# A decoder layer on one Trainium2 core: the second gate/up pair's a12 b21 right behind the first pair's

## The chip, the cores and the metric

The kernel runs on one core of one Trainium2 chip. The metric is the time of one execution in microseconds on the device, the median of several runs. TensorE (PE in the profile) multiplies; VectorE (DVE), ScalarE (ACT) and GpSimd (POOL) work element by element; SyncE (SP) and POOL issue the transfers. Every engine takes its instructions in the order in which they stand in its queue, and waits on semaphores for what others make.

## What is computed

One decoder layer over 512 tokens and 16 meta tokens, of width 2048: an input projection, stick-breaking attention beside a gated short convolution, an output projection with a residual, and then the part that matters here, a SwiGLU feed-forward of width 5632:

```python
        h = h + o @ w_out[l]

        n2 = _rmsnorm(h, g_ffn[l])
        h = h + (jax.nn.silu(n2 @ w_gate[l]) * (n2 @ w_up[l])) @ w_down[l]
```

All of it is float32. TensorE works on fp32r, so each operand is split into hi (a rounded copy) and lo (what is left), and a product is made of three matmuls: hi·hi, hi·lo and lo·hi.

## The kernel before

**Stages.** Input projection and attention, the convolution, the output projection (mostly `wide_product`, lines 709 to 718), then 44 gate/up pairs, then the down projection.

**Seven products for a pair.** A pair `i` is one tile of 128 columns of w_gate and the same of w_up. With the contraction and the 512 tokens cut in two halves each, it is a 2×2 block product, made of seven block products (`block_product`, line 720) instead of eight. In this text product s takes the activations `acts[s]`, named f0 to f6 in the program, and a weight made of the pair's four quads b11, b12, b21, b22 of 128×1024:

| product | weight | accumulates in |
|---|---|---|
| 0 | b11 | x |
| 1 | t1 = b11 + b12 | z |
| 2 | t2 = t1 + b22 | x |
| 3 | b22 | z |
| 4 | t3 = b12 + b22 | x |
| 5 | b21 (the a12 b21) | y |
| 6 | t2 + b21 | x |

Each is 24 matmuls of 256 columns: for each of eight k, hi with the activation's hi (line 736), hi with its lo (737), lo with its hi (738). x, y and z are PSUM banks, two of each. ACT copies banks between products into `sides` (lines 761 to 765), and DVE forms the results (767, 771, 774).

**The weights' way.** SP loads a quad into its place in `sw_in` (line 613). Of six places of 128×1024 four hold quads, the last two the sums: place 4 has t1/t2 and place 5 t3 in even pairs, the other way round in odd ones. DVE adds (648, and in place 682 and 655). For the split of a weight ACT casts hi (641), and DVE subtracts lo (642), into one of three slots of `sw_split`. A split is therefore issued two products ahead, and its cast waits until the product three before is done. The next pair's quad is loaded as soon as the old one is used up; b12, for instance, behind t3.

**Pair 0** takes its products in the order 5, 0, 1, 2, 3, 4, 6 (`FIRST_ORDER`, line 659), since f5 is complete before the others: the last tile of the output projection is that part of the residual stream which f0 to f4 still need. For that tile DVE makes the residual (832 to 835), ACT the source (836), and DVE and ACT the blocks f0, f1, f2 and the last k of f3 and f4. f3, f4 and f6 come back from DRAM by POOL's loads (880), which may start only when the last product of the output projection is done.

**The scale r_h.** h is not normalised before the products. `h_scale` (line 908) makes the factor r_h of each token from the sum of squares acc_h: ACT and POOL split acc_h into work_r (187, 188), two matmuls ss_h sum over the partitions (500, 501), DVE reads them (502), ACT makes Ln and Exp (194, 195) and POOL four operations (196 to 199), which write r_h over acc_h. It is called inside pair 0, ahead of product 4, under high priority. `gate` then multiplies u and g with r_h on DVE (937, 939) and applies Silu on ACT (940, for which ACT loads a table).

**What sets the order.** The program is written in one order; a scheduler moves instructions within an engine's queue by priority and by its own estimate of when their operands are there. `tc.high_priority` lifts the splits and additions. `tc.keep_in_program_order` and `tc.issue_after` hold an instruction to its place.

## Time and profile before

| | |
|---|---|
| median of 3 runs | 2064.36 us (2063.72 to 2064.47) |
| the profiled execution | 2063.57 us, its span 2061.8 us |
| output projection ends, gate/up begins | 792.8 us |
| stretch 792.80 to 800.00: PE, DVE busy | 5.72 and 6.93 of 7.20 us |
| stretch 800.00 to 816.00: PE, DVE busy | 13.36 and 15.53 of 16.00 us |
| stretch 850.00 to 900.00: PE, DVE busy | 50.00 and 46.53 of 50.00 us |

The stretches are read from the view by windows: the first two are those in which TensorE has gaps, the last is a piece of the gate/up products in their steady course. A row of the timeline is start, duration, engine, line, operation, output and input; in brackets stand the idle time ahead of it and what released it.

### The profile page before, as it was taken

The numbers are of one execution on the slowest core, as the hardware profiler recorded it, in microseconds if no ns is written. First come the engines' busy times: TensorE is split into PE (matmuls) and PEld (weight loads), VectorE is DVE, ScalarE is ACT, GpSimd is POOL, SyncE is SP. The second block draws the span as 40 slices with busy tenths as digits, with TensorE's granted clock in tenths as the row PEclk, the third lists the DMA queues.
The fourth block names the chain that finished last, engine by engine and source line by source line (L and its number), as shares of the span: only waits on it lengthen the run. The fifth ranks groups of instructions, "written<-read, shape, count | busy, mean of one in ns | idle before, by whom it ended". The sixth has DMA issues, their size and how long they took to land.

```text
span 2061.8 us, 39364 instructions
## 1 busy us (share of the span) xinstructions
PE 2048.5 (99%) x16086; PEld 1975.5 (96%) x16086; DVE 1629.3 (79%) x2133; ACT 1016.9 (49%) x1522; POOL 368.6 (18%) x499
## 2 busy tenths in 40 slices
PE   9999999999999999999999999999999999999999
PEld 8899999999998888999999999999999999999999
DVE  7877767533336669999898898898888988888888
ACT  7666566322224344555555555555555544444443
POOL 0111111010104544111111011011011243121111
PEclk9999999999999999999999999999999999999999
DMA  5122222222235667546555555465465899798864
GB/s 198 63 82 73 82 72 83 82 93 92 94 104 176 181 187 240 158 135 194 164 145 172 155 163 165 146 180 153 149 175 160 258 332 348 192 296 211 218 149 94
DMA packets 144117, 330.41 MB, mean 160 GB/s; under 512 B 12400, under 2 KB 62064, under 8 KB 143936
## 3 DMA queue, kind: packets, MB, share of 16 engines
q1 hardware_dynamic: 67456, 212.50, 32.2%
q0 software_dynamic: 76480, 115.40, 21.9%
q8 instruction: 126, 2.06, 0.4%
q14 instruction: 55, 0.45, 0.1%
HBM read 260.74 MB, written 67.11 MB: 159 GB/s over the span
## 4 chain that ended last, share of the span: by engine, by line
PE 96%; DVE 2%; DMA 1%; ACT 1%; issue 0%; SPq 0%; POOL 0%; DVEq 0%; ACTq 0%; POOLq 0%
PE x L738 11%; PE x L736 11%; PE x L737 11%; PE z L736 6%; PE z L737 6%; PE z L738 6%; PE y L736 3%; PE y L738 3%; PE y L737 3%; PE po L716 3%; PE po L717 3%; PE po L715 3%; PE pv L173 2%; PE pu L177 1%; PE pc L173 1%; PE pu L173 1%
## 5 line engine op out<-in xcount | busy, mean ns | idle before, releaser
L641 ACT CAST sw_split<-sw_in 128x1024 fp32r<-128x1024 f32 (+1 forms) x534 | 526.6, 988 | 553.0 <-PE z L737 167.0
L642 DVE TENSOR_TENSOR sw_split<-sw_in,sw_split 128x1024 fp32r<-128x1024 f32 (+1 forms) x534 | 615.1, 1152 | 96.7 <-ACT sw_split L641 93.7
L738 PE MATMUL x<-f,sw_split 128*128 128x256 f32 x1408 | 387.8, 275 | 1.7 <-DVE sw_split L642 1.7
L737 PE MATMUL x<-f,sw_split 128*128 128x256 f32 x1408 | 387.7, 275 | 1.3 <-DVE f L188 1.3
L736 PE MATMUL x<-f,sw_split 128*128 128x256 f32 x1408 | 387.7, 275 | 0.2 <-ACT f L187 0.2
L738 PEld LDWEIGHTS x<-f,sw_split 128*128 128x128 f32 x1408 | 264.4, 188 | 1.9 <-DVE sw_split L642 1.9
L737 PEld LDWEIGHTS x<-f,sw_split 128*128 128x128 f32 x1408 | 264.4, 188 | 1.5 <-DVE f L188 1.5
L736 PEld LDWEIGHTS x<-f,sw_split 128*128 128x128 f32 x1408 | 264.4, 188 | 0.5 <-ACT f L187 0.4
L142 DVE TENSOR_TENSOR wlo<-raw,whi 128x512 fp32r<-128x512 f32 (+1 forms) x198 | 139.8, 710 | 124.9 <-ACT whi L141 124.0
L928 POOL DMA_DIRECT2D fd<-s x147 | 103.7, 922 | 690.0 <-DVE s L188 673.5
L141 ACT CAST whi<-raw 128x512 fp32r<-128x512 f32 (+1 forms) x198 | 121.1, 614 | 180.4 <-PE pu L175 64.5
L736 PE MATMUL z<-f,sw_split 128*128 128x256 f32 x704 | 194.0, 276 | 0.6 <-ACT sides L763 0.6
L738 PE MATMUL z<-f,sw_split 128*128 128x256 f32 x704 | 193.9, 275 | 0.0
L737 PE MATMUL z<-f,sw_split 128*128 128x256 f32 x704 | 193.9, 275 | 0.0
L648 DVE TENSOR_TENSOR sw_in<-sw_in 128x1024 f32<-128x1024 f32 (+1 forms) x144 | 166.1, 1153 | 5.4 <-DMA sw_in<-w_down 1.1
L738 PE MATMUL x<-ring,sw_split 128*128 128x256 f32 x608 | 167.5, 276 | 0.5 <-DVE sw_split L642 0.5
L737 PE MATMUL x<-ring,sw_split 128*128 128x256 f32 x608 | 167.4, 275 | 0.0
L736 PE MATMUL x<-ring,sw_split 128*128 128x256 f32 x608 | 167.4, 275 | 0.0
L736 PEld LDWEIGHTS z<-f,sw_split 128*128 128x128 f32 x704 | 132.2, 188 | 0.8 <-ACT sides L763 0.8
L738 PEld LDWEIGHTS z<-f,sw_split 128*128 128x128 f32 x704 | 132.2, 188 | 0.0
L737 PEld LDWEIGHTS z<-f,sw_split 128*128 128x128 f32 x704 | 132.2, 188 | 0.0
L738 PEld LDWEIGHTS x<-ring,sw_split 128*128 128x128 f32 x608 | 114.2, 188 | 0.7 <-DVE sw_split L642 0.7
(345 smaller groups left out, 5256.2 us busy)
## 6 DMA issues: line engine op xcount, KB each, us to landing
sw_in<-w_gu SPq DMA_DIRECT2D x176, 512.0 KB, 3.9
raw<-w_in SPq DMA_DIRECT2D x92, 512.0 KB, 3.3
fd<-s POOLq DMA_DIRECT2D x147, 256.0 KB, 5.4
sw_in<-w_down SPq DMA_DIRECT2D x96, 384.0 KB, 4.1
ring<-fd POOLq DMA_DIRECT2D x42, 768.0 KB, 17.4
sw_in<-w_out SPq DMA_DIRECT2D x30, 512.0 KB, 3.7
out_T<-d POOLq DMA_DIRECT2D x54, 256.0 KB, 4.7
sw_in<-w_down SPq DMA_DIRECT2D x16, 512.0 KB, 7.7
```

The costliest lines, as they stand in the source:

```text
L141: sc.copy(hi[:, :c], raw)
L142: ve.tensor_tensor(lo[:, :c], raw, hi[:, :c].bitcast(F32), ALU.subtract)
L173: pe.matmul(ps, wh, ah[:, a:b], start=k == 0, stop=False)
L641: sc.copy(hi, src)
L642: ve.tensor_tensor(lo, src, hi.bitcast(F32), ALU.subtract)
L648: ve.tensor_tensor(sums[name], a, b, ALU.add)
L715: pe.matmul(ps, hi[:, kk], ah, start=k == 0, stop=False)
L716: pe.matmul(ps, hi[:, kk], al, start=False, stop=False)
L736: pe.matmul(p, hi[:, kk], act[:, 0, k], start=start and j == k == 0, stop=False, skip_group_check=skip)
L737: pe.matmul(p, hi[:, kk], act[:, 1, k], start=False, stop=False, skip_group_check=skip)
L738: pe.matmul(p, lo[:, kk], act[:, 0, k], start=False, stop=k == n - 1, skip_group_check=skip)
L928: gp.dma_start(fd[c][s][:, :, k], t[:, :, i])
```

## The change

Pair 1's product 5 is made right behind pair 0's product 5, both into their own bank y. Its weight b21 is loaded for that a first time, into place 5 of `sw_in`, which is free until t3 of pair 0; the load stands behind the first four loads of the output projection's weights in the text. b21 of pair 1 is loaded again into its own place, for the addition ahead of product 6. The order of splits is a list, `order_w`: (0,5), (1,5), and then all others pair by pair without product 5 of the first two pairs. For pairs 0 and 1 the addition of b21 moves to product 6.

Two orders of issue are set beside it: t3 of pair 1 is kept in program order, and `h_scale` is issued behind the last load of f6.

```diff
     def add_quads(i, name, a, b):
         n = pairs[i][0]
         sums[name] = w_place(sw_in, n, (4 if n == 8 else 6) + ((name == "t3") ^ i % 2))
-        ve.tensor_tensor(sums[name], a, b, ALU.add)
+        return ve.tensor_tensor(sums[name], a, b, ALU.add)
 
     def add_t3(i, b):
-        add_quads(i, "t3", b["12"], b["22"])
+        t3 = add_quads(i, "t3", b["12"], b["22"])
+        if i == 1:
+            tc.keep_in_program_order(t3)
         load_next(i, "12")
...
-    FIRST_ORDER = (5, 0, 1, 2, 3, 4, 6)
+    EARLY = 2
+    order_w = [(i, 5) for i in range(EARLY)] + [
+        (i, s) for i in range(len(pairs)) for s in range(7) if i >= EARLY or s != 5
+    ]
+
+    def load_early():
+        quads["early"] = w_place(sw_in, 8, 5)
+        nc.sync.dma_start(quads["early"], pairs[1][1][2])
...
-        i, s = divmod(len(split_w) - WIDE, 7)
-        if i == len(pairs):
+        if len(split_w) - WIDE == len(order_w):
             return
+        i, s = order_w[len(split_w) - WIDE]
         n = pairs[i][0]
-        if i == 0:
-            s = FIRST_ORDER[s]
...
             elif s == 5:
-                split_quad(b["21"], n)
-                if i:
+                split_quad(quads["early"] if i == 1 else b["21"], n)
+                if i >= EARLY:
                     add_last(i, b)
             else:
-                if not i:
+                if i < EARLY:
                     add_last(i, b)
...
-        y, z, x = bank("y"), bank("z"), bank("x")
+        y, z, x = early.pop(i, None) or bank("y"), bank("z"), bank("x")
         p1, p5, u2 = side("p1"), side("p5"), side("u2")
         if not i:
             block_product(y, acts[5], True)
+            early[1] = bank("y", 1)
+            block_product(early[1], acts[5], True)
         block_product(x, acts[0], True)
...
-        if i:
+        if i >= EARLY:
             block_product(y, acts[5], True)
         ve.tensor_tensor(c1[:, 0], y, p1, ALU.add)
...
     for _ in range(4):
         load_wide()
+    load_early()
...
-                    gp.dma_start(acts[s][:, part, :n], fx[s][:, part, :n], max_dma_last_dim=4096)
+                    last_f = gp.dma_start(acts[s][:, part, :n], fx[s][:, part, :n], max_dma_last_dim=4096)
...
-        with tc.high_priority(1 << 20):
+        with tc.high_priority(1 << 20), tc.issue_after(last_f.ins):
             token_scale(acc_h, acc_h, D, "h", (w[:, 0], w[:, 1], a[:, 0], a[:, 1], b), gp)
```

What this does to the order of instructions is shown at three places. In names, sw_in and sw_split are the weights before and after the split, a number behind x, z, g or u is the pair, and lines of the changed program are 9 to 15 higher.

ScalarE, from the last cast of f3 and f4 to the copy of product 2, before:

```order
L187 CAST f34_8170<-src7_8118 128x256 x2
L641 CAST sw_split_6910<-sw_in_6909 128x1024
L761 COPY sides_8161<-x0_8227 128x256
L641 CAST sw_split_6910<-sw_in_6909 128x1024
L763 COPY sides_8161<-z0_8226 128x256
L187 CAST work_r_8368<-acc_h_6907 128x512
L641 CAST sw_split_6910<-sw_in_6909 128x1024
L765 COPY sides_8161<-x0_8227 128x256
```

And now:

```order
L187 CAST f34_8169<-src7_8117 128x256 x2
L641 CAST sw_split_6910<-sw_in_6909 128x1024
L187 CAST work_r_8396<-acc_h_6907 128x512
L641 CAST sw_split_6910<-sw_in_6909 128x1024
L775 COPY sides_8160<-x0_8226 128x256
L641 CAST sw_split_6910<-sw_in_6909 128x1024
L777 COPY sides_8160<-z0_8225 128x256
```

work_r stood behind the casts for products 3 and 4 and the copies of products 0 and 1; now it stands behind the cast of t2 for product 2, ahead of both.

TensorE, where the first matmul of ss_h stands, before (the end of product 2 of pair 0):

```order
L738 MATMUL x0_8227<-f2_6921,sw_split_6910 128x256
L736 MATMUL x0_8227<-f2_6921,sw_split_6910 128x256
L737 MATMUL x0_8227<-f2_6921,sw_split_6910 128x256
L500 MATMUL ss_h_8373<-work_r_8368,ones_r_104 128x512
L738 MATMUL x0_8227<-f2_6921,sw_split_6910 128x256
```

And now, from the last matmul of product 0:

```order
L747 MATMUL x0_8226<-f0_6919,sw_split_6910 128x256
L745 MATMUL z0_8225<-f1_6920,sw_split_6910 128x256
L746 MATMUL z0_8225<-f1_6920,sw_split_6910 128x256
L747 MATMUL z0_8225<-f1_6920,sw_split_6910 128x256
L745 MATMUL z0_8225<-f1_6920,sw_split_6910 128x256
L746 MATMUL z0_8225<-f1_6920,sw_split_6910 128x256
L747 MATMUL z0_8225<-f1_6920,sw_split_6910 128x256
L745 MATMUL z0_8225<-f1_6920,sw_split_6910 128x256
L500 MATMUL ss_h_8401<-work_r_8396,ones_r_104 128x512
```

It stood behind the 17th matmul of product 2 and now stands behind the seventh of product 1; the second one moves from the fourth matmul of product 3 into product 4. In both programs product 0 of pair 1 begins ahead of product 6 of pair 0 on TensorE.

VectorE, around the read of ss_h (502) and the first use of r_h (937, now 952), before:

```order
L502 TENSOR_SCALAR work_a_8369<-ss_h_8373 128x512
L642 TENSOR_TENSOR sw_split_6910<-sw_in_6909,sw_split_6910 128x1024
L648 TENSOR_TENSOR sw_in_6909<-sw_in_6909 128x1024
L767 SCALAR_TENSOR_TENSOR u0_8224<-z0_8226,sides_8161 128x256
L642 TENSOR_TENSOR sw_split_6910<-sw_in_6909,sw_split_6910 128x1024
L771 SCALAR_TENSOR_TENSOR u0_8224<-x0_8227,sides_8161 128x256
L642 TENSOR_TENSOR sw_split_6910<-sw_in_6909,sw_split_6910 128x1024
L682 TENSOR_TENSOR sw_in_6909<-sw_in_6909 128x1024
L937 TENSOR_TENSOR u0_8224<-u0_8224,acc_h_6907 128x512
L642 TENSOR_TENSOR sw_split_6910<-sw_in_6909,sw_split_6910 128x1024 x2
```

And now:

```order
L781 SCALAR_TENSOR_TENSOR u0_8223<-z0_8225,sides_8160 128x256
L642 TENSOR_TENSOR sw_split_6910<-sw_in_6909,sw_split_6910 128x1024
L502 TENSOR_SCALAR work_a_8397<-ss_h_8401 128x512
L785 SCALAR_TENSOR_TENSOR u0_8223<-x0_8226,sides_8160 128x256
L642 TENSOR_TENSOR sw_split_6910<-sw_in_6909,sw_split_6910 128x1024
L691 TENSOR_TENSOR sw_in_6909<-sw_in_6909 128x1024
L648 TENSOR_TENSOR sw_in_6909<-sw_in_6909 128x1024
L952 TENSOR_TENSOR u0_8223<-u0_8223,acc_h_6907 128x512
L642 TENSOR_TENSOR sw_split_6910<-sw_in_6909,sw_split_6910 128x1024
```

The addition 648 here is t3 of pair 1: it stood ahead of the splits of b11 and t1 of pair 1 and now stands behind both, and behind t2. The read of ss_h has moved from ahead of the split for product 6 of pair 0 to behind that of b11 of pair 1. The multiplication by r_h stands, before and now, right ahead of the split of t2 of pair 1 (before, that of b22 lies between).

On POOL the two loads of f6 move from behind work_r and behind L196 to ahead of work_r. On VectorE the sum t3 of pair 0 and its t2 addition of b22 move too: t3 from behind the split of b21 to behind the split of the second b21, the t2 addition from behind the last residual to behind the blocks f0, f1 and f2.

8 lines of the change are left out of this document (5 added, 3 removed).

## The prediction

> **What bounds the kernel now.** I read the page's head first, then the table of waits cut to the 70 us around the change, then TensorE's timeline there.
>
> ```profile
> span 2061.8 us, 39364 instructions
> PE 2048.5 (99%) x16086; PEld 1975.5 (96%) x16086; DVE 1629.3 (79%) x2133; ACT 1016.9 (49%) x1522; POOL 368.6 (18%) x499
> ...
> PE x L738 <- DVE sw_split L642: 1.7, 1, 1.7
> PE x L737 <- DVE f L188: 1.3, 1, 1.3
> PE ss_h L501 <- POOL work_r L188: 0.9, 1, 0.9
> PE z L736 <- ACT sides L763: 0.6, 1, 0.6
> ```
>
> TensorE is busy for 2048.5 of 2061.8 us, so no change of order can win more than 13.3 us, and most of that is elsewhere. What this change can reach are the four waits shown, all between 792 and 830 us, at the start of the gate/up products. I measure them by the starts of matmuls, because a busy PE has modelled ends.
>
> ```profile
> 792.57 0.39 PE L717 MATMUL po<-oc,sw_split 128*128 128x512 f32 x1
> 792.79 0.28 PE L736 MATMUL y<-f,sw_split 128*128 128x256 f32 x1
> ...
> 798.32 0.38 PE L736 MATMUL x<-f,sw_split 128*128 128x256 f32 x1 [0.22 <-ACT f L187]
> 799.96 0.39 PE L737 MATMUL x<-f,sw_split 128*128 128x256 f32 x1 [1.26 <-DVE f L188]
> ...
> 800.30 0.28 PE L736 MATMUL z<-f,sw_split 128*128 128x256 f32 x1
> ...
> 810.42 0.28 PE L736 MATMUL x<-f,sw_split 128*128 128x256 f32 x1
> ...
> 813.25 0.27 PE L737 MATMUL x<-f,sw_split 128*128 128x256 f32 x1
> 815.22 0.39 PE L738 MATMUL x<-f,sw_split 128*128 128x256 f32 x1 [1.70 <-DVE sw_split L642]
> ...
> 826.76 0.39 PE L736 MATMUL z<-f,sw_split 128*128 128x256 f32 x1 [0.57 <-ACT sides L763]
> ...
> 840.51 0.28 PE L736 MATMUL z<-f,sw_split 128*128 128x256 f32 x1
> ```
>
> From 810.42 to 813.25 there are 25 steps, so 0.113 us a matmul and 2.72 us for a product of 24. A matmul of 512 columns takes 0.22 (792.57 to 792.79). From the first gate/up product at 792.79 to product 1 of pair 2 at 840.51 are 47.72 us; 15 products (40.8) and the two matmuls of ss_h (0.45) are 41.25. So **6.5 us are lost in this stretch**, and they are the whole stake: 0.31% of the kernel. After 840.51 both programs issue the same products in the same order.
>
> **The change part by part.** *Added load.* One more 512 KB on SP, issued in the output projection behind six loads of w_out.
>
> ```profile
> 620.00:640.00 20.00, 20.00 (x88) 16.34 (x87) 10.55 (x13) 7.05 (x9) 5.00 (x6) 1.00 0.43 145
> ```
>
> TensorE has no gap there and the DMA engines are at 0.43, with 150 us until the data is used: 0. Without that cover it would be one landing.
>
> *Moved product.* The number of matmuls is the same, so nothing is removed; 24 of them (2.72 us) go from inside pair 1 to 795.5, into the place where product 0 waited. The question is whether DVE, which feeds all four waits, is also earlier.
>
> *The waits of product 0.* It now starts at 792.79 + 2 × 2.72 = 798.2 and reaches its last k at 800.6.
>
> ```profile
> 793.07 0.69 DVE L832 TENSOR_TENSOR w<-po,acc_a 128x512 f32<-128x512 f32 x1 [0.34 <-PE po L717]
> ...
> 796.00 0.69 DVE L835 TENSOR_TENSOR w<-w,w 128x512 f32<-128x512 f32 x1
> 796.61 1.22 DVE L682 TENSOR_TENSOR sw_in<-sw_in 128x1024 f32<-128x1024 f32 x1
> ...
> 798.41 1.49 DVE L188 TENSOR_TENSOR f<-src,f 128x256 fp32r<-128x256 f32 x1
> ...
> 800.27 0.43 DVE L847 SCALAR_TENSOR_TENSOR src<-src 128x256 f32<-128x256 f32 x1
> 800.62 1.22 DVE L642 TENSOR_TENSOR sw_split<-sw_in,sw_split 128x1024 fp32r<-128x1024 f32 x1
> ...
> 796.73 0.73 ACT L836 ACTIVATE src<-w,vec 128x512 f32<-128x512 f32 x1 [2.91 <-DVE w L835]
> ...
> 798.06 1.56 POOL L207 TENSOR_TENSOR acc_h<-acc_h,w 128x512 f32<-128x512 f32 x1 [3.33 <-ACT w L206]
> ```
>
> On DVE the next operation starts 0.34 after one of 256 columns (800.27 to 800.62), 0.6 after one of 512 (796.00 to 796.61) and some 1.14 after one of 1024, which takes 1.22 itself. The sum for t3 of pair 0 now stands right ahead of the last residual, behind the split of the second b21, so I start the residual at 793.3 (bounds 793.07 as before, and 793.8 if the whole 0.7 of a 512 operation is late). L835 then starts at 796.2, the src activation at 797.0, and the f0 subtraction, which the addition L682 no longer precedes, at 798.7. It ends with POOL's L207, at 800.1, where TensorE comes at 800.6: **both product 0 waits go, 2.1 us** (product 1 started at 800.30, though the 2.72 of product 0 began at 795.51).
> The Trainium skill, "SBUF — State Buffer", section "SBUF: two separate sides", states that VectorE and GpSimd share a port pair as an exclusive lock, so the loser blocks for the other's whole instruction. The 1.49 us of the f0 subtraction against 0.43 for the same size at 800.27, ending 0.28 after POOL's end, agrees. Without such a lock the subtraction would end at 799.1 and the next term would be 0.8 smaller.
>
> *New wait in product 1.* Behind f0, DVE has two 256 operations (0.7) and the split of t1 (1.22): its lo is there at 802.0, where TensorE needs it at 801.2, **0.8**. Then the first ss_h matmul, now behind the seventh matmul of product 1, comes up at 802.6 and needs ACT's work_r. On ACT that stands behind the cast of t2; t2 is added on DVE in the place of t1, so behind the split of t1: f2 0.34 and the addition 1.14 bring 803.5.
>
> ```profile
> 798.17 1.04 ACT L641 CAST sw_split<-sw_in 128x1024 fp32r<-128x1024 f32 x1
> ...
> 804.35 0.62 ACT L187 CAST work_r<-acc_h 128x512 fp32r<-128x512 f32 x1
> ...
> 809.43 0.64 ACT L194 ACTIVATE work_a<-work_a 128x512 f32<-128x512 f32 x1 [1.80 <-DVE work_a L502]
> ...
> 824.53 1.28 ACT L940 ACT_TABLE_LOAD   x1
> 825.82 0.63 ACT L940 ACTIVATE g<-g 128x512 f32<-128x512 f32 x1
> 826.36 0.35 ACT L763 COPY sides<-z 128x256 f32<-128x256 f32 x1
> ```
>
> The cast is done at 804.5, work_r at 805.1: **2.5 us** during which the whole of TensorE's queue stands. Product 1 ends at 807.4, four products and one ss_h matmul done. Before, five products and both were done at 810.42; here that is 807.4 + 2.72 + 0.22 = 810.3. So up to here the moved product has bought nothing: what product 0 no longer waits, product 1 does. Bounds: 2.4 (f0 not held by POOL) to 3.8 (residual 0.5 late) for the two waits together.
>
> *The second wait, at 815.22, goes.* It was the split of pair 1's b11, late behind t3 of pair 1:
>
> ```profile
> 810.97 1.98 DVE L648 TENSOR_TENSOR sw_in<-sw_in 128x1024 f32<-128x1024 f32 x1 [0.43 <-DMA sw_in<-w_gu]
> ...
> 813.20 1.97 DVE L642 TENSOR_TENSOR sw_split<-sw_in,sw_split 128x1024 fp32r<-128x1024 f32 x1
> ...
> 818.89 0.68 DVE L937 TENSOR_TENSOR u<-u,acc_h 128x512 f32<-128x512 f32 x1
> ```
>
> That sum now stands behind two more splits. The two loads of f6, which now stand ahead of work_r in POOL's queue, wait for the last store of out:
>
> ```profile
> out_T<-w SPq DMA_DIRECT2D x1, 256.0 KB, 6.2
> ```
>
> Issued at 797.0, it lands at 803.2; 0.75 each brings 804.7, before ACT's work_r: 0, and without that cover at most 1.5 more at r_h. Products 2, 3 and 4 run without a gap until 815.8 (810.1 + 2 × 2.72 + 0.22). The slot of pair 1's b11 comes free with product 3 at 812.8, cast and split follow at 813.9 and 815.2: in time. Gain 2.0.
>
> *New wait at r_h.* The scale r_h comes from POOL's four operations behind L195. The read of ss_h (L502) now stands behind the b11 split, so at 815.2; L194 follows, then a cast of 1.04 that waits for the end of product 4, then L195 until 818.1.
>
> ```profile
> 810.10 0.63 ACT L195 ACTIVATE work_a<-work_a 128x512 f32<-128x512 f32 x1
> ...
> 810.82 1.03 POOL L196 TENSOR_TENSOR work_b<-work_a 128x512 f32<-128x512 f32 x1 [2.43 <-ACT work_a L195]
> ...
> 815.73 2.15 POOL L199 TENSOR_TENSOR acc_h<-work_a,work_b 128x512 f32<-128x512 f32 x1
> ```
>
> From 810.82 to 817.88 are 7.1 us; the f6 load among them (0.75) is now earlier, so r_h is there at 818.1 + 6.3 = 824.4 instead of 817.9. L937 (line 952 of the change) heads DVE's queue from about 822.5, idle, and behind it stands the split of t2 of pair 1: 0.6 + 1.2 later, 826.2. Products 0 and 6 take TensorE to 815.8 + 5.44 = 821.2, product 1 to 823.9, and the third matmul of product 2 needs that lo at 824.15: **2.0 us**. Bounds: 0.2, with each POOL operation at the 1.03 of L196, when DVE itself is not free before 822.5; and 2.2.
>
> *Silu wait.* Behind that split DVE makes g (0.6); on ACT the table load (1.3), Silu (0.6), a cast (1.0) and the copy of product 1 (0.3) follow, 830.0; product 3 of pair 1 could start at 826.2 + 2.6 = 828.8: **1.2** against 0.7 before (826.76). Both sides start from r_h, so it stays near this: bounds 1.2 and 1.4.
>
> *Pair 2's b11 split.* Behind t2's split DVE has six operations of 1.14, three of 0.6 and two of 0.34 to do, and the split itself: 826.1 + 10.5 = 836.6. TensorE is there at 830.0 + 2 × 2.72 + 0.23 = 835.7: **0.9**; bounds 0, and 2.2 if the b22 for t3 of pair 2 also comes late.
>
> *Sum.* 3.3 + 2.0 + 1.2 + 0.9 = 7.4, and 0.1 for the slower restart at each of five stops, 7.9, against 6.5: +1.4 us. The same adding over the rows of before ends 0.7 later than 840.51, since it holds DVE up by one POOL operation too many; I take half of that off for the changed order, **+1.0 us**. On the profiled execution's 2063.57 that is 2064.6; the runs' median is 0.8 above that execution, so **2065.4 us**. By the bounds: 2.4 + 0.2 + 1.2 + 0 + 0.4 = 4.2, that is -2.3 us, to 3.8 + 2.2 + 1.4 + 2.2 + 0.5 = 10.1, that is +3.6: the forecast's own range is 2062.1 to 2068.0.
>
> **The rivals.** *POOL is quick.* With DVE idle in front of r_h, POOL meets nobody; L196 to L199 take 4.1 instead of 6.3, and DVE goes on at 822.5, 1.9 sooner. All that follows starts from there, so TensorE has the 1.9 too: +1.0 - 1.9 = -0.9, **2063.5**. For it: L196 needed only 1.03. Against: DVE is not idle until 822.5, and L199 took 2.15 beside it.
>
> *The gain stays.* The cast of t2 and work_r come before TensorE asks, r_h too, and only the Silu wait and pair 2's split are left: 1.2 + 0.9 + 0.2 instead of 6.5, -4.2, and with the same correction as above -4.5, **2059.9**. For it: the waits for f0 and for the b11 split, which the order removes, are 4.0 of the 6.5. Against: work_r cannot precede the addition to t2, and the way to 803.5 is made of DVE work that was back to back before.
>
> *DVE stays in debt (the slower side).*
>
> ```profile
> 805.06 2.65 POOL L188 TENSOR_TENSOR work_r<-acc_h,work_r 128x512 fp32r<-128x512 f32 x1 [4.04 <-ACT work_r L187]
> ...
> 830.00:850.00 20.00, 20.00 (x179) 20.00 (x178) 18.25 (x21) 11.03 (x14) 2.09 (x4) 1.00 0.44 133
> ```
>
> If POOL's four operations take the 2.65 of work_r each, r_h comes 4.3 later; DVE, busy 18.25 of 20 us, regains only 1.75 per 20 us, so all of it reaches TensorE: +1.0 + 4.3, **2069.7**. It is slower than the bound once r_h comes later than 827.5. Against: nothing before took POOL that long but work_r.
>
> *The clock.* The 0.8 and 2.5 us in product 1 are parted by only five matmuls. If TensorE's clock is halved behind them, and again behind the wait for r_h, each time for as long as the wait was, half of 3.3 and half of 2.0 us of work are lost: +1.0 + 2.6 = +3.6, **2068.0**. For it nothing but the length: the row of 830 to 850 has a granted clock of 1.00, and so have all stretches of this page, the one with the 1.70 us wait among them.
> The Trainium skill, "TensorE: Matmul & The Clock Gate", section "Part 1: The HAM clock gate (the "warmup" mystery)", states that an idle window of about 3.4 us halves the clock. No wait of this stretch reaches that length, so the trace neither bears it out nor denies it.
>
> **How the numbers follow.** About 0.2% (4.1 us) is what a measurement of this kernel can tell from no change. The forecast 0.51, quick POOL 0.24 and the clock 0.05 lie inside: same 0.80. The gain stays 0.08: faster 0.08. DVE in debt 0.12: slower 0.12. The range goes to just short of 2059.9 below and takes in the bounds and the nearer half of the debt above: 2060.4 to 2069.0.
>
> **What would show it.** In the new trace: no wait of product 0 for f0; a wait of product 1's lo of under 1.3 us, and one of about 2.5 us of the first ss_h matmul for ACT work_r; none at product 0 of pair 1; an idle DVE before the product of u and acc_h, and a wait of 0.2 to 2.2 us for the split behind it. Wrong would be: work_r before 803 (the gain stays), or r_h after 827.5 (the debt). Product 1 of pair 2 should start at 839 to 844.

## The result and the profile after

| | before | changed |
|---|---|---|
| median | 2064.64 us (21 runs, 2063.02 to 2070.01) | 2071.09 us (21 runs, 2069.11 to 2072.47) |
| ratio | | 1.0025 [1.0019, 1.0031] |
| the profiled execution | 2063.57 us | 2069.24 us |
| first gate/up product starts | 792.79 us | 792.59 us |
| from there to product 1 of pair 2 | 47.72 us | 52.54 us |
| of these, work | 41.25 us | 41.25 us |

The change costs 6.5 us by the medians and 0.25%, some 5 us, by the ratio, which goes by all runs; the interval leaves out 1, so the loss is real, though small. The time lies above the predicted range of 2060.4 to 2069.0. Before's own runs spread over 7 us, and the mean granted clock of TensorE goes with it: of the 151 runs of before that were taken beside the experiments, 69 had 1.000 (median 2063.7), 49 had 0.999 (2066.9) and 33 had 0.998 or less (2069.7), while the changed kernel's 21 runs all had 0.997 or 0.998.

Of the profiled execution's 5.67 us, 4.82 were lost in the stretch that the prediction looked at, 1.05 behind it (most of it a wait at 870.33, where there was none), and 0.20 were won ahead of it. The page's head of the changed kernel:

```profile
span 2067.5 us, 39371 instructions
PE 2052.0 (99%) x16086; PEld 1978.7 (96%) x16086; DVE 1626.8 (79%) x2133; ACT 1016.8 (49%) x1522; POOL 368.4 (18%) x499
```

TensorE has the same 16086 matmuls and is busy for 3.5 us longer (2048.5 before). Waits leave an engine idle; they can't make it busier. So something other than waits is in the difference. First the waits, in the table from 780 us on (engine and line, what it waited for, us in total, times, longest):

```profile
PE ss_h L500 <- ACT work_r L187: 2.6, 1, 2.6
PE x L747 <- DVE sw_split L642: 2.4, 2, 2.1
PE z L747 <- DVE sw_split L642: 1.1, 1, 1.1
PE z L745 <- ACT sides L777: 0.6, 1, 0.6
```

The four waits of before for f0, for work_r on POOL, for the split of b11 and for the Silu are gone or moved; these have come in their place. TensorE's timeline has them with their times:

```profile
792.59 0.28 PE L745 MATMUL y<-f,sw_split 128*128 128x256 f32 x1
...
798.07 0.28 PE L745 MATMUL x<-f,sw_split 128*128 128x256 f32 x1
...
801.05 0.28 PE L745 MATMUL z<-f,sw_split 128*128 128x256 f32 x1
...
802.52 0.38 PE L747 MATMUL z<-f,sw_split 128*128 128x256 f32 x1 [1.07 <-DVE sw_split L642]
...
806.00 0.50 PE L500 MATMUL ss_h<-work_r,ones_r 128*128 128x512 f32 x1 [2.63 <-ACT work_r L187]
...
829.21 0.39 PE L747 MATMUL x<-f,sw_split 128*128 128x256 f32 x1 [2.05 <-DVE sw_split L642]
...
839.76 0.39 PE L747 MATMUL x<-f,sw_split 128*128 128x256 f32 x1 [0.31 <-DVE sw_split L642]
...
845.13 0.28 PE L745 MATMUL z<-f,sw_split 128*128 128x256 f32 x1
```

From 792.59 to 801.05 no row has a wait in brackets: both y products and product 0 run through, as meant. Then product 1 stops twice and product 2 of pair 1 once. The brackets in the stretch sum to 6.06 us (4.70 before). What the brackets don't show stands in the windows behind two of them (columns: stretch, its length, busy us of PE, PEld, DVE, ACT, POOL, then TensorE's granted clock, DMA share, GB/s):

```profile
806.70:810.10 3.40, 3.40 (x19) 3.40 (x18) 3.32 (x3) 0.84 (x3) 0.77 (x1) 0.50 1.22 414
830.70:833.20 2.50, 2.50 (x13) 2.33 (x13) 2.46 (x5) 2.33 (x5) 0.00 (x0) 0.50 0.38 125
```

TensorE is busy all the time and does 19 matmuls in 3.40 us, where 30 fit in at 0.113 each: **the clock is halved behind the wait of 2.63 and again behind the one of 2.05**. In each place some 15 matmuls start 0.213 us apart instead of 0.113, about 3.0 us in both. Before, behind its wait of 1.70 at 815.22, the same columns have a full clock:

```profile
815.20:820.00 4.80, 4.78 (x41) 4.78 (x42) 4.77 (x5) 1.32 (x2) 2.60 (x2) 1.00 0.87 339
```

The waits themselves are made where the prediction put them. ACT's timeline of the changed kernel around work_r:

```profile
804.02 1.04 ACT L641 CAST sw_split<-sw_in 128x1024 fp32r<-128x1024 f32 x1 [1.95 <-DVE sw_in L691]
805.33 0.62 ACT L187 CAST work_r<-acc_h 128x512 fp32r<-128x512 f32 x1 [0.27 <-DMA out_T<-w]
805.86 1.04 ACT L641 CAST sw_split<-sw_in 128x1024 fp32r<-128x1024 f32 x1
806.80 0.37 ACT L775 COPY sides<-x 128x256 f32<-128x256 f32 x1
```

work_r waits behind the cast of t2, which waited 1.95 for the addition; and then another 0.27 for the landing of the last store of out, since the tile of work_r lies over the memory from which that store reads (experiment 5 takes this away). DVE's timeline, from the read of ss_h to the first use of r_h:

```profile
817.66 0.68 DVE L502 TENSOR_SCALAR work_a<-ss_h 128x512 f32<-128x512 f32 x1
...
821.24 1.95 DVE L691 TENSOR_TENSOR sw_in<-sw_in 128x1024 f32<-128x1024 f32 x1
823.11 2.33 DVE L648 TENSOR_TENSOR sw_in<-sw_in 128x1024 f32<-128x1024 f32 x1
827.33 0.69 DVE L952 TENSOR_TENSOR u<-u,acc_h 128x512 f32<-128x512 f32 x1 [1.90 <-POOL acc_h L199]
```

And POOL's, the four operations that make r_h:

```profile
820.56 1.54 POOL L196 TENSOR_TENSOR work_b<-work_a 128x512 f32<-128x512 f32 x1 [13.09 <-ACT work_a L195]
822.18 2.17 POOL L197 TENSOR_TENSOR work_b<-work_b,work_a 128x512 f32<-128x512 f32 x1
824.45 1.47 POOL L198 TENSOR_SCALAR work_b<-work_b 128x512 f32<-128x512 f32 x1
826.00 1.30 POOL L199 TENSOR_TENSOR acc_h<-work_a,work_b 128x512 f32<-128x512 f32 x1
```

The scale r_h is complete at 827.3, against 817.9 before, and DVE stands idle for it.

### The profile page after: what moved, and what is told of

Its sections match the earlier page's. It is cut to its first block, busy times and chain, and to the rows that moved or that the text cites. A ratio compares the mean times of both kernels' runs of the same rounds, so it can differ in the third digit from the quotient of the medians.

```text
span 2067.5 us, 39371 instructions
## 1 busy us (share of the span) xinstructions
PE 2052.0 (99%) x16086; PEld 1978.7 (96%) x16086; DVE 1626.8 (79%) x2133; ACT 1016.8 (49%) x1522; POOL 368.4 (18%) x499
## 3 DMA queue, kind: packets, MB, share of 16 engines
q8 instruction: 126, 2.06, 0.4%
## 4 chain that ended last, share of the span: by engine, by line
PE 92%; DVE 3%; issue 2%; ACT 1%; POOL 1%; DMA 1%; DVEq 0%; POOLq 0%; ACTq 0%
PE x L747 11%; PE x L745 11%; PE x L746 11%; PE z L745 5%; PE z L746 5%; PE z L747 5%; PE y L745 3%; PE y L746 3%; PE y L747 3%; PE po L725 2%; PE po L726 2%; PE po L724 2%; PE pv L173 2%; PE pu L177 1%; PE pc L173 1%
```

## The experiments

All kernels are the changed one with one edit, unless a heading says that they are before with one edit. The runs of before in the batches had medians of 2066.47 (1 to 4), 2064.93 (5 to 8), 2066.43 (9 to 12), 2066.64 (13 to 16) and 2064.72 (17 and 18), and those of before's runs at a clock of 1.000 lay between 2063.55 and 2064.45 in all five, so medians from different batches can be set beside each other to about a microsecond.

**1. The scale behind product 2.** ss_h's first matmul may not stand in product 1 any more.

```diff
...
-        block_product(x, acts[2], False)
+        last_mm[0] = block_product(x, acts[2], False)
...
-        with tc.high_priority(1 << 20), tc.issue_after(last_f.ins):
+        with tc.high_priority(1 << 20), tc.issue_after(last_f.ins), tc.issue_after(last_mm[0].ins):
```

> The changed kernel with one row moved: the first matmul of ss_h is issued behind the last matmul of product 2 of pair 0, instead of behind the seventh of product 1; all other orders are the changed kernel's. Theory (waits of TensorE's queue and the halved clock behind them): the 2.9 us gap at that matmul goes and with it the 1.6 us that the halved clock took behind it; the split of t2 then comes about 1.0 us late for product 2. The scale r_h follows the products, so its wait in product 2 of pair 1 stays near 2.3 with a halved clock of 1.2 us behind. Product 1 of pair 2 starts at about 841.6 instead of 845.1; the time is 3.5 us lower, 2067.6. Rival (VectorE's row of splits sets the end of the stretch, and TensorE only chooses where it waits): the next split takes all of it, product 1 of pair 2 starts at 844.5 to 845.5, the time is 2070.5 to 2071.5.

Measured: 2067.80 (2067.03 to 2070.49), ratio 1.0010 [1.0001, 1.0019]. The forecast of the median holds. The profiled execution is the highest of its runs and shows that the wait wasn't taken away: TensorE now waits behind product 1, for the copy that stands behind work_r on ACT. Work_r itself waited 1.16, which its row puts down to the load of an f. ACT's timeline there:

```profile
806.86 0.62 ACT L187 CAST work_r<-acc_h 128x512 fp32r<-128x512 f32 x1 [1.16 <-DMA f<-fx]
...
808.33 0.36 ACT L775 COPY sides<-x 128x256 f32<-128x256 f32 x1
```

TensorE's row at the start of product 2:

```profile
808.75 0.39 PE L745 MATMUL x<-f,sw_split 128*128 128x256 f32 x1 [2.81 <-ACT sides L775]
```

And the windows behind this wait and behind the one for r_h:

```profile
808.70:812.40 3.70, 3.65 (x18) 3.66 (x19) 3.67 (x4) 1.21 (x2) 0.65 (x1) 0.54 1.19 406
830.00:833.00 3.00, 2.80 (x22) 2.60 (x22) 3.00 (x5) 2.27 (x3) 0.00 (x0) 1.00 0.13 22
```

The wait of 2.81 is again followed by a halved clock; that of 2.06 at 830.09, the wait for r_h, this time is not. Eight of the 11 runs lie at 2067.0 to 2068.0 with a clock of 0.999 or 1.000.

**2. TensorE kept busy through the first wait.** The wait stays, but 24 matmuls of f5 with ones, into a bank that nobody reads, run ahead of ss_h's first matmul. The rest of the edit defines `filler` and holds ss_h's two matmuls to the places that they have in the changed kernel.

```diff
...
+            with tc.high_priority(1 << 20), tc.issue_after(mms[3, 2].ins):
+                last = filler(24) if 24 else mms[3, 2]
+            with tc.high_priority(1 << 20), tc.issue_after(last.ins):
+                pe.matmul(ps, ones_r, w[:, 0], start=True, stop=False)
...
```

> The changed kernel with 24 more matmuls of 256 columns into an unused bank of PSUM, issued right ahead of the first matmul of ss_h, so that TensorE works while it would have waited for work_r; the orders of the other engines are the changed kernel's. Theory (the clock halves because TensorE stood still): the records show a full clock from 806 to 810, product 2 starts 1.5 us earlier, the halved stretch behind the wait for r_h stays, the time is 1.5 us lower, 2069.6. Rival (the clock has another cause, or its cost is hidden behind later waits): the stretch stays halved, or the next wait grows by as much: 2070.6 to 2071.6, or up to 1 us slower if the 24 matmuls last longer than the wait.

Measured: 2069.22 (2068.60 to 2070.95), 1.0014 [1.0005, 1.0023]. TensorE's timeline:

```profile
804.16 3.00 PE L926 MATMUL fill<-f,ones_r 128*128 128x256 f32 x24
807.00 0.40 PE L947 MATMUL ss_h<-work_r,ones_r 128*128 128x512 f32 x1
```

And the windows behind both waits:

```profile
807.00:811.00 4.00, 4.00 (x36) 3.95 (x35) 3.96 (x5) 2.17 (x4) 1.43 (x1) 1.00 1.20 413
828.50:832.00 3.50, 3.48 (x20) 3.48 (x21) 3.46 (x5) 2.85 (x4) 0.00 (x0) 0.65 0.23 51
```

ss_h comes no earlier in its product, but the clock behind it is full; only the second place is still halved. For useless work the kernel takes 1.5 to 1.9 us less than the changed one (2070.67 and 2071.09): this part of the loss is the clock's, not the wait's. The transfers aren't the cause either: the DMA share is 1.20 here at full clock, and was 1.22 at half.

**3. Both waits filled.** Experiment 2 with 20 more such matmuls ahead of the lo that waits behind r_h. From there on the orders of VectorE and ScalarE differ a little from the changed kernel's.

```diff
...
+                if used[0] - 1 - WIDE == order_w.index((1, 2)) and k == 0:
+                    filler(20, mid)
...
```

> As the run before, and 20 such matmuls more ahead of the third matmul of product 2 of pair 1, where TensorE waits for the split that stands behind r_h (from there on the orders of VectorE and ScalarE differ a little from the changed kernel's in pairs 1 and 2). Theory: no halved stretch is left, the mean clock is 1.000, product 1 of pair 2 starts 2.7 us earlier at 842.4, the time is 2068.4, and the runs lie closer together. Rival: as for the run before, 2070.6 to 2071.6.

Measured: 2068.27 (2067.51 to 2069.08), 1.0007 [0.9998, 1.0016], the clock 1.000 in nearly every run, as expected. That is 2.4 to 2.8 us less than the changed kernel, and the clock's share may be somewhat larger, since two waits that it hides (1.00 for a copy of z, 1.22 for a lo of pair 2) come back at full clock.

**4. The use of r_h behind t2 of pair 1.** DVE takes the split of t2 ahead of the first multiplication by r_h.

```diff
...
+        if first_gate:
+            with tc.issue_after(lo_at[order_w.index((1, 2))].ins):
+                first_gate()
         block_product(z, acts[1], True)
...
```

> The changed kernel with the gate of pair 0 written inside pair 1, so that on VectorE the product of u and r_h stands behind the split of t2 of pair 1 instead of ahead of it. Theory (that split is held by r_h): the wait of 2.3 us in product 2 of pair 1 goes with the halved clock of 1.2 behind it, and the split of b22, now the first behind r_h, comes about 1.0 late for product 3: 2.5 us lower, 2068.6. Rival (r_h only passes its wait on to the next split): product 1 of pair 2 starts at 844.5 to 845.5 and the time is 2070.5 to 2071.5.

Measured: 2070.32 (2069.18 to 2071.58), 1.0021 [1.0012, 1.0030]; the rival is the nearer one, the median 0.2 under its range. The wait of 2.05 is gone, and three of about a microsecond have come: for the split of b22, for a copy, and for a split of pair 2. A late r_h is paid somewhere. In the profiled execution the halved stretch behind work_r also has 23 steps, where the changed kernel's first profile has 15. TensorE's rows:

```profile
832.40 0.39 PE L747 MATMUL z<-f,sw_split 128*128 128x256 f32 x1 [1.13 <-DVE sw_split L642]
...
836.21 0.39 PE L745 MATMUL x<-f,sw_split 128*128 128x256 f32 x1 [0.99 <-ACT sides L782]
...
840.46 0.38 PE L747 MATMUL x<-f,sw_split 128*128 128x256 f32 x1 [0.99 <-DVE sw_split L642]
```

**5. A smaller work_r.** The tile of work_r has two rows instead of five and no longer lies over the memory of the last store.

```diff
-        w = apool.tile([P, 5, SEQ], F32R, tag="s5", name="work_r")
+        w = apool.tile([P, 2, SEQ], F32R, tag="s5", name="work_r")
```

> The changed kernel with work_r made as a tile of two rows of 512 instead of five, in the same place, so that it no longer lies over the memory from which the last tile of out is stored; every order is the changed kernel's. Theory (on ScalarE work_r waits for that store to land, by 0.3 us in the profiled run and by more in others, and all of TensorE's queue with it): the wait at the first matmul of ss_h is 2.3 to 2.4 in every run, the runs lie closer together and the median falls by 1 to 2 us, to 2069.6. Rival (the cast of t2 alone sets work_r): 2070.6 to 2071.6.

Measured: 2069.96 (2068.86 to 2070.87), 1.0019 [1.0011, 1.0028]. The median is 0.7 to 1.1 below the changed kernel's, between the theory and the rival. On ACT work_r no longer waits for a transfer; TensorE's wait for it is 2.27 instead of 2.63, and behind it the clock is halved as before (10 steps). So the store's landing is a real cause, of 0.3 us in this pair of profiles; most of the wait is the place behind the cast.

**6. work_r behind the copy, too.** Experiment 1 with work_r also behind the copy of product 1 on ACT.

```diff
...
-        sc.copy(p5, z)
+        last_mm[1] = sc.copy(p5, z)
...
-        with tc.high_priority(1 << 20), tc.issue_after(last_f.ins), tc.issue_after(last_mm[0].ins):
+        with tc.high_priority(1 << 20), tc.issue_after(last_f.ins), tc.issue_after(last_mm[0].ins), tc.issue_after(last_mm[1].ins):
```

> The changed kernel with ss_h behind product 2 as in the run hold_ss, and with work_r on ScalarE behind the copy of product 1 instead of ahead of the copies of products 0 and 1. Theory (what stands behind work_r on ScalarE is held by it too: in the run hold_ss the copy of product 0 was, and product 2 waited 2.8 us for it): the waits are 1.3 in product 1 and about 1.0 in product 2, with a full clock to 820; the wait of about 2 us for r_h in pair 1 stays. Product 1 of pair 2 starts some 49.3 us after the first gate/up product (52.5 in the changed kernel); the median is 2067.3 and the runs lie closer than those of hold_ss. Rival (VectorE's row of splits sets the end): 2070 to 2071.

Measured: 2066.88 (2066.20 to 2067.48), 1.0007 [0.9999, 1.0016], clock 0.999 to 1.000, and the stretch is 49.5 us (49.3 expected). Six waits of 0.77 to 1.07 us are left, 5.73 in all, and none longer: almost the changed kernel's sum of waits (6.06) at full clock, and some 4 us less in time.

**7. Experiment 6 with the small work_r, and the scale not behind f6's loads.**

```diff
-        with tc.high_priority(1 << 20), tc.issue_after(last_f.ins), tc.issue_after(last_mm[0].ins), tc.issue_after(last_mm[1].ins):
+        with tc.high_priority(1 << 20), tc.issue_after(last_mm[0].ins), tc.issue_after(last_mm[1].ins):
```

> As the run hold_both, with the small work_r, and with h_scale no longer issued behind the last load of f6; with that the second matmul of ss_h comes up in product 3 instead of 4 and the read of ss_h stands two splits earlier on VectorE, and so does the product of u and r_h. Theory: r_h is there some 5 us earlier, its wait in pair 1 goes with the halved clock behind it, and about 1 us of it comes back at the next splits: the stretch is 47 us, the mean clock 1.000, the median 2065.0. Rival (r_h passes its wait on, as it did when the gate of pair 0 was made later): 2067 to 2068.

Measured: 2068.27 (2066.21 to 2068.88), 1.0007 [0.9997, 1.0017]: the rival. r_h came 6 us earlier, and the scheduler moved its use forward by more, so DVE stood idle for it for 4.07 us, and behind that a copy made TensorE wait 2.68 us, with a halved clock behind it. DVE's row:

```profile
821.29 0.69 DVE L952 TENSOR_TENSOR u<-u,acc_h 128x512 f32<-128x512 f32 x1 [4.07 <-POOL acc_h L199]
```

**8. Before, with the small work_r.** The edit of experiment 5.

```diff
-        w = apool.tile([P, 5, SEQ], F32R, tag="s5", name="work_r")
+        w = apool.tile([P, 2, SEQ], F32R, tag="s5", name="work_r")
```

> The kernel before, with the small work_r; every order is that of the kernel before. Theory (the runs of the kernel before at 2067 to 2070, all with a mean clock under 1.000, are those in which the last store of out lands late, so that TensorE waits longer for work_r and its clock is halved): all runs lie at 2063 to 2066, the median at 2064.3. Rival (their clock has another cause): the runs spread as before, median 2066 to 2067.

Measured: 2068.18 over 12 runs, from 2063.37 to 2070.54, 1.0009 [0.9999, 1.0019]. The expectation falls: four runs lie at 2063 to 2065.4 and seven at 2068 to 2070.5, the same spread as before's. So the tile of work_r does not make it.

**9. All three.** Experiment 7 with the late use of r_h of experiment 4.

```diff
...
-        with tc.high_priority(1 << 20), tc.issue_after(last_f.ins):
+        with tc.high_priority(1 << 20), tc.issue_after(last_mm[0].ins), tc.issue_after(last_mm[1].ins):
...
+            with tc.issue_after(lo_at[order_w.index((1, 2))].ins):
+                first_gate()
...
```

> As the run small_hold_early, and the gate of pair 0 written inside pair 1 as in the run late_gate, so that the read of ss_h stays early on VectorE while the product of u and r_h stands behind the split of t2 of pair 1. Theory (of the two only both together take the wait away: an early r_h alone was followed by an equally early use of it, a late use alone by the next split): VectorE stands less than 0.5 us before that product, no wait of TensorE is over 1.5 us, the mean clock is 1.000, the stretch from the first gate/up product to product 1 of pair 2 is 46.5 us against 52.5 in the changed kernel and 47.7 in the kernel before; the median is 2064.0, below the kernel before's. Rival (the waits of about 1 us at the copies and at the splits only change places, and the load of f6 lands late): 49 us as in the run hold_both, 2066.5 to 2068.

Measured: 2067.55 (2066.00 to 2068.47), 1.0002 [0.9993, 1.0011]. The theory's 2064.0 is missed and the rival's range of 2066.5 to 2068 holds: the gate is now so late that product 3 of pair 1 waits 2.62 us for the copy behind the Silu, and the clock is halved for some 4 us behind it.

**10. Before, with its wait of 1.70 filled.** 14 of the useless matmuls ahead of the lo of b11.

```diff
...
+                if used[0] - 1 - WIDE == 7 and k == 0:
+                    filler(14)
...
```

> The kernel before with 14 more matmuls of 256 columns into an unused bank, ahead of the matmul that waits 1.7 us for the split of b11 of pair 1, so that TensorE works while it would have waited (on VectorE one product of pair 0's gate moves by a split). Theory (the runs of the kernel before at 2067 to 2070 are those in which this wait, or one like it, halves the clock): every run has a mean clock of 1.000 and lies at 2063 to 2066. Rival (their clock falls elsewhere): runs spread from 2063 to 2070 as before.

Measured: 2066.11 (2064.18 to 2070.42, 12 runs), 0.9999 [0.9988, 1.0011]. Five runs of 12 still lie at 2068.4 or higher. 1.6 us of fillers don't cover what happens in those runs; experiment 16 shows a wait that is longer.

**11. The scale free, t3 held.** The changed kernel without its second order of issue.

```diff
-        with tc.high_priority(1 << 20), tc.issue_after(last_f.ins):
+        with tc.high_priority(1 << 20):
```

> The changed kernel without the issue of h_scale behind the last load of f6. The second matmul of ss_h comes up in product 2 instead of 4, the read of ss_h stands three splits earlier on VectorE, and so do the first use of r_h (now ahead of the split of t1 of pair 1) and the loads of f6 stand behind work_r again. Theory (the wait at the first matmul of ss_h is set by work_r, which does not move; r_h is earlier, but so is its use): the first wait stays at 2.6 with its halved clock, the wait for r_h moves one product ahead and stays near 2 us: 2070 to 2071.5. Rival (this order of issue costs the time): the wait for r_h goes, 3.5 us lower, 2067.6.

Measured: 2066.98 (2065.28 to 2068.03), 1.0001 [0.9992, 1.0010]. The theory falls and the rival holds: this one line is worth 3.7 to 4.1 us. The read of ss_h stands 5.3 us earlier and r_h is there at 821.7 instead of 827.3. DVE's timeline:

```profile
812.34 0.69 DVE L502 TENSOR_SCALAR work_a<-ss_h 128x512 f32<-128x512 f32 x1 [2.24 <-PE ss_h L501]
...
821.73 0.69 DVE L952 TENSOR_TENSOR u<-u,acc_h 128x512 f32<-128x512 f32 x1 [0.94 <-POOL acc_h L199]
```

And the window behind TensorE's first wait:

```profile
806.60:812.20 5.60, 5.60 (x24) 5.41 (x25) 3.49 (x3) 2.46 (x4) 2.71 (x2) 0.50 0.87 289
```

The split behind L952 makes TensorE wait no more, and the second halved stretch goes with that wait. The first wait is still there (3.27 us for work_r, of which 0.90 is the landing of the store on ACT), with 5.6 us at half clock behind it. Half of that, 2.8 us, is an estimate of what the clock still costs here; experiment 14 wins 1.1 of it.

**12. t3 free, the scale held.** The changed kernel without its first order of issue.

```diff
-            tc.keep_in_program_order(t3)
+            pass
```

> The changed kernel without the order that keeps t3 of pair 1: on VectorE it stands three splits earlier, ahead of the split of b22's successor as before the change. Theory: the split of b11 of pair 1 is late again, by 1 to 2 us, and what stands between it and the use of r_h is shorter by the same 1.2 to 2.3, while r_h itself, behind that split, is 1.2 later: the wait for r_h is no smaller and the time is 1 to 2 us higher, 2072 to 2073. Rival (the addition had free time there): 2070.5 to 2071.6.

Measured: 2071.42 (2070.48 to 2073.28), 1.0025 [1.0016, 1.0033]; its median is within the rival's range and below the theory's. In the profiled execution, at 2072.31 one of the longer ones, r_h comes at 828.6, 1.3 later, as the theory had it. Beside the changed kernel's 2070.67 and 2071.09 the order of t3 is worth less than 0.8 here.

**13. The use of r_h held at another place.** Experiment 6 with the small work_r; pair 0's multiplications by r_h stand behind the split of b22 of pair 1 and the copy of its product 2.

```diff
...
+        if gate_0:
+            with tc.issue_after(lo_at[order_w.index((1, 3))].ins), tc.issue_after(u2_copy.ins):
+                gate_0()
...
```

> As the run hold_both, with the small work_r, and with all of pair 0's gate that uses r_h held on VectorE behind the split of b22 of pair 1 and on ScalarE behind the copy of product 2 of pair 1; the read of ss_h stays where the changed kernel has it. Theory (the late r_h costs by what stands behind its first uses: a split on VectorE, copies on ScalarE): with both behind it, VectorE does not stand before the product of u and r_h, no wait in pair 1 is over 1 us, the stretch from the first gate/up product to product 1 of pair 2 is 46.5 us (47.7 before, 52.5 changed, 49.5 hold_both), the mean clock 1.000, the median 2064. Rival (VectorE's sum of work up to pair 2 sets the end, wherever the waits stand): 49 us, 2066.5 to 2067.

Measured: 2066.58 (2065.59 to 2067.89), 0.9999 [0.9990, 1.0008], where the theory had 2064: the rival's time. There are again four waits (1.07, 1.01, 1.60 for f6's load, 1.58 for a lo of pair 2). Behind the 1.58 the clock was halved, behind the 1.60 not.

**14. The scale free, and the first wait filled.** Experiment 11 with the small work_r and 22 fillers.

```diff
...
+            with tc.issue_after(mms[3, 2].ins):
+                last = filler(22)
+            with tc.issue_after(last.ins):
+                pe.matmul(ps, ones_r, w[:, 0], start=True, stop=False)
+            with tc.issue_after(mms[4, 1].ins):
+                pe.matmul(ps, ones_r, w[:, 1], start=False, stop=True)
...
```

> As the run no_hold_h, with the small work_r and with 22 more matmuls of 256 columns into an unused bank ahead of the first matmul of ss_h. Theory (behind that wait 5 us of work run at half the clock, 2.5 us lost, and r_h follows TensorE there, since VectorE waited 2.2 us for the second matmul of ss_h): no halved stretch, every run at a mean clock of 1.000, median 2.3 us under no_hold_h, 2064.7. Rival (the use of r_h, now ahead of the split of t1 of pair 1, becomes the wait): 2066.5 to 2067.5.

Measured: 2065.85 (2065.25 to 2067.80), 0.9999 [0.9990, 1.0008], clock 0.999 to 1.000, between the theory's 2064.7 and the rival's 2066.5, and 1.1 under experiment 11. It is the best form of the moved product that was found, and no faster than before.

**15. The changed kernel again, unaltered.**

> The changed kernel itself, beside the others on one chip. Theory: a median of 2071.1 as in its first 21 runs, mean clock 0.997 to 0.998 in every run. Rival (its first runs were made on a chip on which it was slower): 2069 to 2070.

Measured: 2070.67 (2069.26 to 2071.93), 1.0021 [1.0013, 1.0030], and a second profile, of 2070.64 us. The median lies between the theory's 2071.1 and the rival's 2070, and the clock is 0.997 or 0.998 in every run. The windows of the profile behind the two long waits (2.67 and 2.05):

```profile
806.80:812.60 5.80, 5.80 (x30) 5.70 (x30) 4.40 (x4) 1.99 (x4) 0.93 (x1) 0.55 1.20 408
830.70:833.20 2.50, 2.50 (x22) 2.49 (x22) 2.50 (x3) 1.99 (x3) 0.00 (x0) 1.00 0.00 0
```

The same kernel: this time 24 steps of 0.213 us behind the first wait (15 in the other execution), and none behind the second.

**16. Before again, one execution.**

> The kernel before itself, one execution. If it is one at 2067 or over: theory, a wait of TensorE between 792 and 840 is longer than in the first profile by 1 us or more, with a granted clock of 0.5 for some 5 us behind it; rival, no longer wait there, and the halved clock stands behind the waits of 1.3 or 1.7 us that the first profile has too, or elsewhere in the kernel. If it is one at 2063 to 2065, it tells nothing.

Measured: 2068.80 us at a clock of 0.998, so it is one of before's longer executions, and it shows what makes this one longer. DVE's row of t3 of pair 1:

```profile
812.98 2.87 DVE L648 TENSOR_TENSOR sw_in<-sw_in 128x1024 f32<-128x1024 f32 x1 [1.55 <-DMA sw_in<-w_gu]
```

TensorE's, at the lo of b11:

```profile
817.45 0.58 PE L738 MATMUL x<-f,sw_split 128*128 128x256 f32 x1 [3.76 <-DVE sw_split L642]
```

And the window behind it:

```profile
817.40:823.00 5.60, 5.55 (x28) 5.55 (x29) 4.04 (x4) 0.46 (x1) 1.13 (x1) 0.55 0.57 197
```

t3 of pair 1 waited 1.55 for the loads (0.43 in the profile of before) and took 2.87 (1.98); the split of b11 behind it was late by 3.76 instead of 1.70, and behind that the clock was halved for 22 steps. The stretch to product 1 of pair 2 is 51.68 us instead of 47.72.

**17. Before, with t3 of pair 1 held.** Of the whole change only the first order of issue.

```diff
...
-        add_quads(i, "t3", b["12"], b["22"])
+        t3 = add_quads(i, "t3", b["12"], b["22"])
+        if i == 1:
+            tc.keep_in_program_order(t3)
```

> The kernel before with the change's order of t3 of pair 1 alone: on VectorE that sum stands two splits later, behind those of b11 and t1 of pair 1; all other engines' orders are the kernel before's. Theory (in its runs at 2067 to 2070 the load of b12 lands late, t3 holds VectorE and with it the split of b11, and the clock halves behind the wait): the wait at the third matmul of pair 1's product 0 is under 0.5 us, every run has a mean clock of 1.000 and lies at 2062 to 2065, the median at 2063. Rival (the late load holds the split behind t3's new place as much): runs at 2063 to 2070 as before.

Measured: 2063.40 (2062.68 to 2064.08 in ten runs at a clock of 1.000, and one of 2069.60 at 0.998), 0.9993 [0.9984, 1.0003]. As expected, but for that one run, of which there is no profile. The wait for the split of b11 is gone from the table of waits:

```profile
PE x L739 <- DVE f L188: 1.3, 1, 1.3
PE x L739 <- DMA f<-fx: 1.0, 1, 1.0
PE ss_h L501 <- POOL work_r L188: 1.0, 1, 1.0
PE z L738 <- ACT sides L765: 0.6, 1, 0.6
```

Its median is the lowest of all, 1.3 us under before's; the interval includes 1, so it is not shown to be faster.

**18. Before, with the scale held.** Of the whole change only the second order of issue.

```diff
...
-        with tc.high_priority(1 << 20):
+        with tc.high_priority(1 << 20), tc.issue_after(last_f.ins):
```

> The kernel before with the change's other order alone: h_scale issued behind the last load of f6, by which the second matmul of ss_h moves from product 3 into product 0 of pair 1 and its read on VectorE three splits back. Theory (this order makes r_h late, and that is most of the changed kernel's loss: without it the changed kernel was 4.1 us faster): r_h is some 5 us later, TensorE waits about 2 us more in pair 1, the clock falls behind it; the runs that lie at 2063.5 in the kernel before lie at 2066 to 2067, the median 2 to 4 us over the kernel before's. Rival (the order costs only beside the early product): a median within 1 us of the kernel before's.

Measured: 2066.99 (2065.84 to 2067.40), 1.0008 [0.9999, 1.0017], the median 2.3 above before's, in the expected place, by another way than expected. The interval just includes 1; but none of its 11 runs is below 2065.84, and 13 of before's 21 are. The two loads of f6 now go out ahead of work_r, and in that execution b12 landed late for t3. DVE's timeline:

```profile
813.99 1.23 DVE L648 TENSOR_TENSOR sw_in<-sw_in 128x1024 f32<-128x1024 f32 x1 [4.13 <-DMA sw_in<-w_gu]
...
818.62 0.69 DVE L502 TENSOR_SCALAR work_a<-ss_h 128x512 f32<-128x512 f32 x1 [0.47 <-PE ss_h L501]
```

TensorE waited 2.90 us for the split of b11, with a halved clock behind it. r_h was late too (L502 at 818.62), but nothing waited for it here.

**What the three parts are worth.** By the medians: before 2064.6; with t3 held alone 2063.4; with the moved product as well 2067.0 (11); with the scale held behind f6's loads too, the changed kernel, 2070.7 and 2071.1. So the order of t3 gains about 1.3 (not shown: the interval of experiment 17 includes 1), the moved product costs about 3.6 (2.4 with its wait filled and the small work_r, 14), and holding the scale costs 3.7 to 4.1. The parts don't simply add: in before, holding the scale costs 2.3 (18), and beside the moved product and the held scale the order of t3 is worth less than 0.8 (12).

## Why the prediction was wrong, step by step

**The waits of product 0: right.** Both are gone, and product 1 starts at 801.05 (predicted: 798.2 + 2.72 = 800.9).

**The new waits in product 1: right.** 1.07 for the lo of t1 (predicted 0.8) and 2.63 for work_r behind the cast of t2 (predicted 2.5). Part of the second is the store's landing, which wasn't in the prediction: its sentence on the f6 loads looked at that store only as POOL's cover.

**The wait for the split of b11: right.** It is gone, and experiment 17 shows that t3's order alone removes it.

**r_h: right in size, later in time.** The wait is 2.05 (predicted 2.0), but r_h came at 827.3 instead of 824.4. L502 was read 2.5 us later than predicted, since the splits ahead of it wait for products that end later: product 1 ended at 809.65 instead of 807.4, and 1.5 of that is the first halved stretch. POOL's four took 6.7 (predicted 6.3). TensorE was late as well, so the difference is the same. DVE in debt, the slower rival, needed r_h after 827.5. At 827.3 it nearly came to that point, but not by its mechanism: POOL's operations took 1.30 to 2.17, not 2.65. Quick POOL is refuted by the same rows, 6.7 where it had 4.1.

**Silu and pair 2: too high.** Instead of 1.2 and 0.9 there is hardly a stop at product 3, and one of 0.31. Where the clock is full at this place, 1.00 and 1.22 are there (experiment 3), 1.01 and 0.76 (experiment 1) or 1.00 and 0.75 (experiment 15): with a halved clock the other engines have more time. For the kernel that the prediction imagined these two terms were nearly right.

**The restart: too low.** It was taken as 0.1 for each stop. The matmul at 802.52 starts 1.35 behind the one ahead of it, of which 1.07 are the wait and 0.11 a step; and the next starts 0.22 later, another 0.11 lost: 0.28 for each stop.

**The clock: the step that failed.** The prediction gave it 0.05, because "For it nothing but the length" spoke and all stretches of the profile of before stood at 1.00, the one with 1.70 us of wait among them. That was one execution with no single wait above 1.70, used as evidence on waits of 2.0 and 2.5. The clock was halved in the changed kernel in both profiles, and its mean was below full in all of its runs. As a mechanism and nearly as a price the rival was right: half of 3.3 and half of 2.0, 2.6 us, against 3.0 in the profile and 2.4 to 2.8 by the median of experiment 3. Its rule for the length, as long as the wait, isn't borne out: some 15 steps stand behind both waits. With 3.0 for the clock the forecast of 2065.4 would have been 2068.4, inside the stated range. The Trainium skill's rule ("TensorE: Matmul & The Clock Gate", section "Part 1: The HAM clock gate (the "warmup" mystery)") was read as a threshold of 3.4 us for a single wait; the runs here halve the clock behind 2.05, so by this reading they differ from it, and the measurement decides.

**The sum.** The stretch lost 11.3 us (52.54 less 41.25), and the prediction had 7.5 (7.9 less the 0.4 taken off). The 3.8 between are the clock, +3.0; restarts, +0.6; the correction by 0.4 that wasn't there; some 1.1 in steps that no row names; and waits, -1.3. Behind the stretch and ahead of it come 0.85, which the prediction had as nothing. And the median lies 1.85 above the profiled execution, not 0.8: that execution was one of the lowest of its kernel. The one of experiment 15, at 2070.64, is nearer to the median: it starts the products 0.27 later, and its stretch is 53.63 us, with 7.53 of waits instead of 6.06, though with 24 halved steps in all instead of some 30. 3.8 + 0.85 + 1.05 = 5.7, the distance from 2065.4 to 2071.09.

**What the prediction left out.** It costed the two orders of issue as a part of the moved instructions and never asked what each alone does. Experiments 11, 17 and 18 do: the order of t3 costs nothing and perhaps gains, and the held scale costs as much as the moved product. The prediction had the wait for a late r_h (2.0) in its sum, but not that it comes from the second order: without that order the wait of 2.05 and the halved stretch behind it are gone, and 3.7 to 4.1 us with them.

**What stays open.** Which part of a single run's time each halved stretch makes can't be told from medians. Nor is it settled why nine of experiment 1's 11 runs have a clock of 0.999 or 1.000 although its one profile, of its longest run, shows a wait of 2.81 with a halved clock behind it. About 1.1 us of the changed kernel's stretch is in no row. Whether t3's order alone is faster than before (0.9993 [0.9984, 1.0003]) would need more runs.

## What to carry to other kernels

When a product is moved into a place where TensorE waits, ask what the same engines were to do for the product behind it: here every microsecond won at product 0 came back at product 1, one cast further on. Price a long wait as the wait and the half clock behind it; in this kernel that holds for all waits from 2.27 us and for some from 1.58. Several waits of a microsecond cost less than one of their sum, as experiment 6 shows beside the changed kernel (5.73 us in six waits, a stretch of 49.5, against 6.06 in four and 52.5). Where a change brings an order of issue along, take it apart and measure each piece: the gain of one can be hidden by the loss of the other.

## What the runs showed of the hardware

**The clock falls behind short waits, and not always.** In all profiles of this study, from the first gate/up product on, single waits of TensorE of up to 1.26 us were never followed by a halved clock, unless a long one came next. Of 1.51 (experiment 10), 1.58 and 1.60 (13), 1.70 (before) and 1.71 (8) only the 1.58 was. Of the five of 2.05 or 2.06, three were (the changed kernel's first profile, 2 and 5) and two not (1 and 15). All twelve from 2.27 to 3.76 were, some with a wait of 1.07 shortly ahead, some alone. A halved stretch lasted from about 2 to 5.6 us, whatever the wait's length, and costs half of that. The Trainium skill, in the section named above, also states that the window in which activity is counted runs freely; that the same wait has a halved clock behind it in one execution and none in the next agrees with this, but no row shows the window.

**Useless matmuls pay.** 24 matmuls that nobody reads, in a wait that stays, take 1.5 to 1.9 us off the changed kernel (experiment 2), as they keep its clock up; in before (experiment 10), 14 of them took off nothing that can be measured; they last 1.6 us, and in the longer execution of experiment 16 the wait is 3.76.

**The spread of before's runs has a cause in the kernel.** In the two executions whose profiles are here it is one split behind one addition that waits for a load: 0.43 or 1.55 us for the load, 1.70 or 3.76 at TensorE, full clock or half. With that addition held back, ten of 11 runs lie within 1.4 us; what made the eleventh longer isn't shown.
